# A mixture-of-experts stage with each pair's gate and up products one step ahead of its down products, and five pairs of eight through a table in DRAM

## The chip, the cores and the metric

The kernel runs on one core of a Trainium2 chip. The metric is the device time of one execution in microseconds; a time that stands for a kernel is the median of its runs. The rows come from one profiled execution, and their time starts at the beginning of its span.

## The reference

Two layers, each a token mixer and a mixture of experts, on 256 tokens of 1024 channels, all in float32. The change concerns the experts alone (16 of them with an inner width of 256; each token takes two experts of one group of four):

```python
def moe_ffn(h, w_router, b_router, w_gate, w_up, w_down):
...
    _, local = lax.top_k(in_group, TOP_K_EXPERTS)
...
    gate = jnp.einsum('tk,tke->te', wts, jax.nn.one_hot(expert_idx, N_EXPERTS, dtype=jnp.float32))
    hid = jax.nn.silu(jnp.einsum('td,edf->tef', h, w_gate)) * jnp.einsum('td,edf->tef', h, w_up)
    hid = hid * gate[:, :, None].astype(hid.dtype)
    return jnp.einsum('tef,efd->td', hid, w_down)
...
        y = moe_ffn(h.reshape(bsz * seq, d), w_router, b_router, w_gate[l], w_up[l], w_down[l])
        x = layer_norm(DEEPNORM_ALPHA * x + (1.0 + g_f) * y.reshape(bsz, seq, d), ln_ffn_g[l], ln_ffn_b[l])
```

## The kernel before

The experts of a layer are worked through as eight pairs `p` (`E // 2`). Of a pair, each expert has 64 slots for tokens, so that the two lie side by side on 128 partitions. Per layer the pairs read 33.6 MB of gate and up weights (`w_gu`, 8 loads of 0.524 MB for a pair) and 16.8 MB of down weights (`w_dn`, 4 such loads for a pair).

For each pair the code does this:

- **Gathering** (L1096 to L1111, `gather`): matmuls of 128x256 with a one-hot matrix `oh` bring the tokens of two pairs (`q = p // 2`) into their slots, transposed. One call makes 8 matmuls into a PSUM bank of tag `t` and lets ScalarE (L208) and VectorE (L1110) write two of the eight blocks of `xg`. Four calls, 32 matmuls, serve two pairs. For pairs 4 and 6 they are recorded in the pair ahead (`AHEADP = ((3, 5), (3, 5))`), for pair 2 between its own products.
- **Gate and up products** (L1205): 16 instructions, each run as two matmuls, into one bank of tag `s`.
- **Activation**: three calls on ScalarE (L208), two on VectorE (L1235, L1236).
- **Two transposes** (L1238), a copy by ScalarE to `hdT` (L1240), and **down products** (L1253): 8 instructions, two halves `n` of 512 columns.
- **Output.** For `p < DIRECT = 6`, VectorE multiplies (L1257) and GpSimd stores the half into a table in DRAM (L1258, 0.262 MB a store). Pairs 6 and 7 go directly: one-hot rows (`slot_rows`, L1218), a multiply (L1265), a split into two parts (L418, L419), and matmuls L1278 that add into the four banks `py`.
- **Table rows** (L1148 to L1159, `table_rows`, recorded at `p == DIRECT`): four indirect loads by GpSimd (L1154, 0.524 MB each) read the two rows of every token, and VectorE adds them to `xrow` (eight sums, L1159). At the end `xrow` is added into `py` (L1273, L1274) and the layer norm follows.

The weights come through `Stream`: SP issues all loads (L92) in one list (built at L167 to L189), which for each pair names the gate and up weights and then the down weights. Each load waits until its buffer's last reader is done. Tag `P`, for down weights, has six buffers, tag `ring` has ten. SP executes in order, so that a load that waits holds up all behind it.

A scheduler sets the order of instructions on each engine from the recorded program and priorities; it may move an instruction ahead of one that was recorded earlier. PSUM has four banks of tag `mm`, two of `s`, two of `t`.

Of the kernel before, what the change touches and what calls it, by code (L numbers as in the profile page):

```python
# [11 lines left out]
F32R = mybir.dt.float32r  # L12
# [25 lines left out]

DIRECT = 6

AHEADP = ((3, 5), (3, 5))

# [70 lines left out]
def _trunk(ctx, tc, x_tok, x_chn, par, pos, rows, b_ada, w_ada, w_idx, w_in, w_out, w_gu, w_dn, out):  # L113
# [30 lines left out]
    for l in range(L):  # L144
# [32 lines left out]
        st.add(("gu", l, 2), w_gu[l, 2], 8, which=range(2, 7))  # L177
        for p in range(2, E // 2):
            if p in SP[l]:
                st.add(("gu", l, p), w_gu[l, p], 8, which=range(2))  # L180
                st.add(("gu2", l, p), w_gu[l, p], 4, "S", (2,))
                st.add(("gu", l, p), w_gu[l, p], 8, which=(2, 3, 6, 7))
            elif p > 2:
                st.add(("gu", l, p), w_gu[l, p], 8)
            if p in DNS[l]:
                st.add(("dn", l, p), w_dn[l, p], 4, "P", (0, 1))
                st.add(("dn2", l, p), w_dn[l, p], 2, "S", (1,))
            else:
                st.add(("dn", l, p), w_dn[l, p], 4, "P")  # L189
    norm_rows(2 * L - 1)  # L190
# [666 lines left out]
    for l in range(L):  # L857
# [237 lines left out]

        def gather(xg, q, k0):  # L1096
            pt = ps("t")
            for j in range(2):
                k = k0 + j
                for tt in range(2):  # L1100
                    for i, src in enumerate((xh, xl)):
                        last = PE.matmul(pt[:, j * 256:(j + 1) * 256], src[:, tt * D + k * P:tt * D + (k + 1) * P],  # L1102
                                  oh[:, tt * D + q * 256:tt * D + (q + 1) * 256], start=(tt + i == 0), stop=(tt + i == 2))
            for j in range(2):
                k = k0 + j
                o, t = xg[:, k * 256:(k + 1) * 256], pt[:, j * 256:(j + 1) * 256]
                if j == 0:
                    act(o, t, AF.Identity, scale=gp[:, k:k + 1], bias=bp[:, k:k + 1])
                else:
                    V.tensor_scalar(o, t, gp[:, k:k + 1], bp[:, k:k + 1], op0=OP.mult, op1=OP.add)  # L1110
            return last  # L1111

        xg = sb("S")
        gl = gather(xg, 0, 0)
        for (la, na), q in zip(LAST[l], pa):
# [64 lines left out]

        for p in range(E // 2):
            pgu = ps("s")
            if p and p % 2 == 0 and p - 1 not in AHEADP[l]:
                xg = sb("S")
            elif p % 2 == 0 and p:
                xg = xnext
            if p in AHEADP[l]:
                xnext = sb("S")

            order = (2, 3, 0, 1) if p == 1 else range(4)  # L1190
            for i in order:
                if p == 0 and i or p and p % 2 == 0 and p - 1 not in AHEADP[l]:
                    gather(xg, p // 2, 2 * i)
                if p in AHEADP[l]:
                    gather(xnext, p // 2 + 1, 2 * i)
                if ("gu2", l, p, i) in st.index:
# [5 lines left out]
                for k in range(2):  # L1202
                    for s in range(2):
                        c0 = (2 * i + k) * 256 + p % 2 * P + s * 64
                        PE.matmul(pgu[s * 64:s * 64 + 64, :], xg[:, c0:c0 + 64], ws[s][k],  # L1205
                                  start=(i == order[0] and k == 0), stop=(i == order[3] and k == 1), tile_position=(0, 64 * s))
            if p == 0:
                sgate = slot_gates()
            if p == 1:
                with tc.issue_after(stored.ins):  # L1210
                    affine_rows(xrow, xn, 2 * l, True)
            if p == DIRECT:
                py = [[ps("mm") for _ in range(2)] for _ in range(2)]
                table_rows()
            def slot_rows(pt):

                for s in range(2):
                    PE.matmul(pt[s * 64:s * 64 + 64, 256:512], identb[:, 2 * p + s:2 * p + s + 1].to_broadcast([P, 64]), rankz,  # L1218
                              start=True, stop=True, tile_position=(0, 64 * s))
                ohT = sb("e", F32R)[:, 0:256]  # L1220
                V.tensor_scalar(ohT, pt[:, 256:512], pidx, None, op0=OP.is_equal)
                return ohT

            late = LATE_ROWS[l] or p < DIRECT
            if LATE_ROWS[l]:
                pt = pgu
            else:
                pt = ps("t")
            if not late:
                ohT = slot_rows(pt)  # L1230
            si = sb("rope")[:, 0:256]
            act(si, pgu[:, 0:256], AF.Exp, scale=-1.0)
            act(si, si, AF.Ln, bias=ones)
            act(si, si, AF.Exp, scale=-1.0)
            V.scalar_tensor_tensor(si, pgu[:, 0:256], sgate[:, p:p + 1], si, op0=OP.mult, op1=OP.mult)  # L1235
            V.tensor_tensor(si, pgu[:, 256:512], si, op=OP.mult)  # L1236
            for j in range(2):
                PE.transpose(pt[:, j * P:(j + 1) * P], si[:, j * P:(j + 1) * P], ident)  # L1238
            hdT = sb("sg")[:, 0:256].rearrange("p (j t) -> p j t", j=2)
            A.copy(hdT, pt[:, 0:256].rearrange("p (j t) -> p j t", j=2))  # L1240
            if late and p >= DIRECT:
                ohT = slot_rows(pt)
            for n in range(2):
# [4 lines left out]
                else:  # L1248
                    wd = [parts_of(("dn", l, p, 2 * n + s)) for s in range(2)]
                pyb = ps("t" if p >= DIRECT else "mm")  # L1250
                for k in range(2):
# [117 lines left out]
```

## Time and profile before

| | us |
|---|---|
| median of 3 runs | 732.42 |
| lowest and highest | 731.96, 732.84 |
| the profiled execution | 735.13 |
| its span | 733.4 |
| TensorE busy | 662.6 (90%) |
| VectorE busy | 404.1 (55%) |

The experts of layer 0 run from about 242 to 375 us of the span, those of layer 1 from about 592 to the end. A busy share is an average over stages with different limits, so the stages are read one by one: windows tell what is busy in a stretch, the waits of SP tell whether a load was held up by a reader of its buffer or by earlier loads that had not landed, and the chain of waits tells which work ended last.

### The profile page before, as it was taken

How to read it: one execution, taken by the hardware profiler on the slowest of the kernel's cores; microseconds unless marked ns; L12 is line 12 of the kernel's file. 1: busy time of each engine (PE TensorE's matmuls, PEld its weight loads, DVE VectorE, ACT ScalarE, POOL GpSimd, SP SyncE). 2: the span in 40 equal slices, each digit the busy share in tenths (PEclk: the TensorE clock that was granted, in tenths of full speed). 3: DMA queues.
4: the chain of work that ended last, by engine and by line, in shares of the span. 5: the costliest groups of instructions: out<-in, count | busy, mean ns of one | idle time of the engine just before them, and what ended most of it. 6: DMA issues, size and time to landing. Idle time of an engine off the chain costs nothing. (4 is left out here: it accounts for less than half of the span.)

```text
span 733.4 us, 10314 instructions
## 1 busy us (share of the span) xinstructions
PE 662.6 (90%) x3578; PEld 402.0 (55%) x3578; DVE 404.1 (55%) x882; ACT 274.2 (37%) x571; POOL 209.7 (29%) x207
## 2 busy tenths in 40 slices
PE   5899699999998999999778999999799799999863
PEld 0567587864775443442246679886377644434222
DVE  5478996653985322221387999664745622222236
ACT  3346658344323212120146646844432222211112
POOL 5003934001922054003034513400830304510201
PEclk9999989999897999999989999999989699999997
DMA  8997773499987799999944774439958569999971
GB/s 305 408 365 239 259 259 119 150 364 409 384 294 252 272 371 339 374 414 412 409 181 142 253 250 147 155 100 373 368 209 255 198 230 329 344 367 412 412 287 57
DMA packets 58849, 210.25 MB, mean 287 GB/s; under 512 B 6948, under 2 KB 7076, under 8 KB 57511
## 3 DMA queue, kind: packets, MB, share of 16 engines
q1 hardware_dynamic: 55152, 198.49, 74.2%
q0 software_dynamic: 3200, 10.50, 3.6%
q8 instruction: 30, 0.49, 0.3%
q10 hardware_dynamic: 438, 0.54, 0.2%
q14 instruction: 29, 0.23, 0.1%
HBM read 202.15 MB, written 7.35 MB: 286 GB/s over the span
## 5 line engine op out<-in xcount | busy, mean ns | idle before, releaser
L419 DVE TENSOR_TENSOR sb_w<-sb_ring,sb_w 128x512 fp32r<-128x512 f32 (+1 forms) x156 | 121.5, 791 | 40.5 <-ACT sb_w L418 39.2
L418 ACT CAST sb_w<-sb_ring 128x512 fp32r<-128x512 f32 (+1 forms) x156 | 92.2, 608 | 82.2 <-PE ps_mm L438 43.6
L1205 PE MATMUL ps_s<-sb_ring,sb_S 128*64 128x512 f32 x424 | 118.3, 611 | 4.5 <-DMA sb_ring<-w_gu 4.2
L437 PE MATMUL ps_mm<-sb_w,sb_H 128*128 128x512 f32 (+2 forms) x224 | 81.3, 368 | 1.1 <-ACT sb_w L418 0.7
L438 PE MATMUL ps_mm<-sb_w,sb_H 128*128 128x512 f32 (+2 forms) x224 | 79.5, 357 | 2.9 <-DVE sb_H L891 2.8
L439 PE MATMUL ps_mm<-sb_w,sb_H 128*128 128x512 f32 (+2 forms) x224 | 73.7, 372 | 2.1 <-DVE sb_w L419 2.0
L1205 PEld LDWEIGHTS ps_s<-sb_ring,sb_S 128*64 128x64 f32 x424 | 32.2, 138 | 65.3 <-issue 44.6
L920 POOL TENSOR_TENSOR sb_ring<-sb_ring,sb_g 128x512 f32<-128x512 f32 x32 | 46.8, 1500 | 66.9 <-DMA sb_ring<-w_out 66.9
L1258 POOL DMA_DIRECT2D table<-sb_e x24 | 13.4, 558 | 174.0 <-DVE sb_e L1257 154.4
L352 PE MATMUL ps_t<-sb_ring,cact 128*32 128x512 f32 x272 | 46.1, 616 | 8.2 <-DVE cact L218 6.7
L1110 DVE TENSOR_SCALAR sb_S<-ps_t,afffg,afffb 128x256 f32<-128x256 f32 x32 | 17.4, 544 | 62.0 <-ACT sb_S L208 62.0
L439 PEld LDWEIGHTS ps_mm<-sb_w,sb_H 128*128 128x128 f32 x224 | 40.8, 194 | 15.4 <-DVE sb_w L419 6.7
L437 PEld LDWEIGHTS ps_mm<-sb_w,sb_H 128*128 128x128 f32 x224 | 42.8, 193 | 11.4 <-issue 3.1
L438 PEld LDWEIGHTS ps_mm<-sb_w,sb_H 128*128 128x128 f32 x224 | 43.0, 193 | 8.9 <-DVE sb_H L891 3.6
L1253 PE MATMUL ps_mm<-sb_P,sb_sg 128*64 128x512 f32 x176 | 46.2, 597 | 0.7 <-ACT sb_sg L1240 0.5
L1102 PEld LDWEIGHTS ps_t<-sb_O,sb_H 128*128 128x128 f32 x256 | 33.0, 193 | 19.0 <-issue 13.0
L208 ACT ACTIVATE sb_S<-ps_t,afffb,afffg 128x256 f32<-128x256 f32 x32 | 18.1, 564 | 62.3 <-PE ps_t L1102 62.3
L438 PE MATMUL ps_mm<-sb_H,sb_w 128*128 128x256 f32 x128 | 37.2, 291 | 3.9 <-DVE sb_w L419 3.9
L531 POOL TENSOR_TENSOR sb_rope<-sb_rope 128x256 f32<-128x256 f32 (+1 forms) x16 | 14.2, 888 | 92.7 <-DVE iwm L567 32.7
L636 POOL TENSOR_SCALAR sb_sg<-sb_sg,sm 128x128 f32<-128x128 f32 (+1 forms) x32 | 27.6, 880 | 45.6 <-DVE sm L633 31.7
L1102 PE MATMUL ps_t<-sb_O,sb_H 128*128 128x256 f32 x256 | 38.7, 297 | 1.8 <-DVE sb_O L1032 1.8
L1235 DVE SCALAR_TENSOR_TENSOR sb_rope<-ps_s,sgate,sb_rope 128x256 f32<-128x256 f32 x16 | 7.7, 482 | 53.1 <-ACT sb_rope L208 53.1
(368 smaller groups left out, 1243.8 us busy)
## 6 DMA issues: line engine op xcount, KB each, us to landing
sb_ring<-w_gu SPq DMA_DIRECT2D x106, 512.0 KB, 7.0
sb_ring<-w_ada SPq DMA_DIRECT2D x96, 512.0 KB, 5.7
sb_P<-w_dn SPq DMA_DIRECT2D x58, 512.0 KB, 11.4
sb_ring<-w_in SPq DMA_DIRECT2D x56, 512.0 KB, 4.4
sb_ring<-w_out SPq DMA_DIRECT2D x16, 512.0 KB, 10.0
sb_S<-w_gu SPq DMA_DIRECT2D x6, 1024.0 KB, 5.7
table<-sb_e POOLq DMA_DIRECT2D x24, 256.0 KB, 6.5
sb_row<-rows SPq DMA_DIRECT2D x8, 512.0 KB, 10.2
```

What stands on the lines that cost most here:

```text
L208: return A.activation(o, i, f, bias=bias, scale=scale)
L352: PE.matmul(pa[32 * g:32 * g + 32, :], cact[:, k:k + 1].to_broadcast([P, 32]), w[g // 2][:, (g % 2) * 512:(g % 2) * 512 + 512], start=(i = ...
L418: A.copy(hi, src)
L419: V.tensor_tensor(lo, src, hi.bitcast(F32), op=OP.subtract)
L437: PE.matmul(o, a[0], b[0], start=start, stop=False)
L438: PE.matmul(o, a[1], b[0], start=False, stop=False)
L439: return PE.matmul(o, a[0], b[1], start=False, stop=stop)
L636: G.tensor_scalar(sg[:, i * n:(i + 1) * n], sg[:, i * n:(i + 1) * n], sm[:, h:h + 1], None, op0=OP.mult)
L920: G.tensor_tensor(q, q, g1[l][0][:, n * 512:(n + 1) * 512], op=OP.mult)
L1102: last = PE.matmul(pt[:, j * 256:(j + 1) * 256], src[:, tt * D + k * P:tt * D + (k + 1) * P], oh[:, tt * D + q * 256:tt * D + (q + 1) * 25 ...
L1205: PE.matmul(pgu[s * 64:s * 64 + 64, :], xg[:, c0:c0 + 64], ws[s][k], start=(i == order[0] and k == 0), stop=(i == order[3] and k == 1), ti ...
L1253: PE.matmul(pyb[s * 64:s * 64 + 64, :], hdT[:, k, s * 64:s * 64 + 64], wd[s][k], start=(k == 0), stop=(k == 1), tile_position=(0, 64 * s))
```

## The change

- The loop over pairs becomes a loop over nine steps. A step records the gate and up products of pair `step` and their activation, then, for pair `p = step - 1`, the transposes, the copy, the whole gathering for pair `p + 2` (where `p` is even), and the down products. `AHEADP` is gone.
- The gathering for pairs 0 and 1 is recorded ahead of their products (the first call aside, which was there before).
- `gather` uses banks of tag `mm` (its first call `t`), the down products of all pairs `t`.
- The list of weights names the gate and up weights of pair `p` ahead of the down weights of pair `p - 1`.
- `DIRECT` is 5: five pairs are stored in the table, pairs 5, 6 and 7 go directly.

```diff
-DIRECT = 6
-
-AHEADP = ((3, 5), (3, 5))
+DIRECT = 5
...
-        for p in range(2, E // 2):
-            if p in SP[l]:
+        for p in range(3, E // 2 + 1):
+            if p == E // 2:
+                pass
+            elif p in SP[l]:
...
-            if p in DNS[l]:
-                st.add(("dn", l, p), w_dn[l, p], 4, "P", (0, 1))
+            if p - 1 in DNS[l]:
+                st.add(("dn", l, p - 1), w_dn[l, p - 1], 4, "P", (0, 1))
...
-        def gather(xg, q, k0):
-            pt = ps("t")
+        def gather(xg, q, k0, tag="mm"):
+            pt = ps(tag)
...
-        for p in range(E // 2):
+        def gate_up(p):
+
             pgu = ps("s")
-            if p and p % 2 == 0 and p - 1 not in AHEADP[l]:
-                xg = sb("S")
-            elif p % 2 == 0 and p:
-                xg = xnext
-            if p in AHEADP[l]:
-                xnext = sb("S")
...
+        for i in range(1, 4):
+            gather(xg, 0, 2 * i)
+
+        now = []
+        for step in range(E // 2 + 1):
+            if step < E // 2:
+                pgu = gate_up(step)
+                if step == 0:
+                    sgate = slot_gates()
+                now.append((pgu, activation(step, pgu)))
+            if step == 0:
+                continue
+            p = step - 1
+            pgu, si = now.pop(0)
+            pt = pgu if LATE_ROWS[l] else ps("t")
+            for j in range(2):
+                PE.transpose(pt[:, j * P:(j + 1) * P], si[:, j * P:(j + 1) * P], ident)
+            hdT = sb("sg")[:, 0:256].rearrange("p (j t) -> p j t", j=2)
+            A.copy(hdT, pt[:, 0:256].rearrange("p (j t) -> p j t", j=2))
+            if p % 2 == 0 and p < E // 2 - 2:
+                xg = sb("S")
+                for i in range(4):
+                    gather(xg, p // 2 + 1, 2 * i)
...
-                pyb = ps("t" if p >= DIRECT else "mm")
+                pyb = ps("t")
```

In the changed program the lines move: gate and up products L1196, activation L1205 and L1206 on VectorE, transposes L1234, copy L1236, down products L1259, multiply and store L1263 and L1264, direct products L1284, loads on SP L90. The lines up to L1166 that are named above (L1102, L1154, L1159) keep their numbers.

**TensorE, layer 1, around pair 2's down products.** Before, from the gathering behind pair 1's down products on (`sb_O` is the one-hot gathering's operand, `sb_sg` is `hdT`, `sb_P` the down weights, `ident` marks transposes):

```order
L1102 MATMUL ps_t<-sb_O,sb_H 128x256 x16
L1205 MATMUL ps_s<-sb_ring,sb_S 64x512 x4
L1205 MATMUL ps_s<-sb_S 64x512 x4
L1205 MATMUL ps_s<-sb_ring,sb_S 64x512 x4
L1102 MATMUL ps_t<-sb_O,sb_H 128x256 x5
L1238 MATMUL ps_s<-ident,sb_rope 128x128 x2
L1102 MATMUL ps_t<-sb_O,sb_H 128x256 x11
L1253 MATMUL ps_mm<-sb_P,sb_sg 64x512 x8
L1205 MATMUL ps_s<-sb_ring,sb_S 64x512 x7
```

After:

```order
L1259 MATMUL ps_t<-sb_w,sb_sg 64x512
L1196 MATMUL ps_s<-sb_ring,sb_S 64x512 x8
L1196 MATMUL ps_s<-sb_S 64x512 x4
L1196 MATMUL ps_s<-sb_ring,sb_S 64x512 x4
L1234 MATMUL ps_s<-ident,sb_rope 128x128 x2
L1102 MATMUL ps_mm<-sb_O,sb_H 128x256 x24
L1259 MATMUL ps_t<-sb_P,sb_sg 64x512 x8
L1196 MATMUL ps_s<-sb_ring,sb_S 64x512 x16
L1234 MATMUL ps_s<-ident,sb_rope 128x128 x2
```

The down products of pair 2 stand behind 24 gather products that follow its transposes; counted from the start of the layer's experts, 104 gather products stand ahead of them, before 88. In layer 0 the same count is 64 before and 88 after, and two more gate and up instructions of pair 4.

**SP, layer 1, the loads of the experts from their third pair on.** Before:

```order
L92 DMA sb_O<-w_gu 128x2048
L92 DMA sb_ring<-w_gu 128x1024 x10
L92 DMA sb_S<-w_gu 128x2048
L92 DMA sb_P<-w_dn 128x1024 x4
L92 DMA sb_ring<-w_gu 128x1024 x2
L92 DMA sb_P<-w_dn 128x1024 x2
L92 DMA sb_ring<-w_gu 128x1024 x9
L92 DMA sb_P<-w_dn 128x1024 x4
L92 DMA sb_ring<-w_gu 128x1024 x8
```

After:

```order
L90 DMA sb_O<-w_gu 128x2048
L90 DMA sb_ring<-w_gu 128x1024 x10
L90 DMA sb_S<-w_gu 128x2048
L90 DMA sb_P<-w_dn 128x1024 x4
L90 DMA sb_ring<-w_gu 128x1024 x5
L90 DMA sb_P<-w_dn 128x1024 x2
L90 DMA sb_ring<-w_gu 128x1024 x6
L90 DMA sb_P<-w_dn 128x1024 x4
L90 DMA sb_ring<-w_gu 128x1024 x8
```

Two down loads move back by three ring loads; the four down loads that go into the buffers freed by pair 2's down products (the last row but one) keep their place in the stream of bytes. So does the last gate and up load of each layer, which is followed by four down loads (2.1 MB) in layer 1 and two (1.0 MB) in layer 0.

**TensorE, layer 1, late: pairs 4 and 5.** Before, from pair 5's transposes (the last stored pair) to pair 6's transposes:

```order
L1238 MATMUL ps_s<-ident,sb_rope 128x128 x2
L1205 MATMUL ps_s<-sb_ring,sb_S 64x512 x3
L1253 MATMUL ps_mm<-sb_P,sb_sg 64x512 x4
L1205 MATMUL ps_s<-sb_ring,sb_S 64x512 x8
L1253 MATMUL ps_mm<-sb_P,sb_sg 64x512 x4
L1238 MATMUL ps_s<-ident,sb_rope 128x128 x2
```

After, from the last gate and up products ahead of pair 4's down products (now the last stored pair) to pair 5's first:

```order
L1196 MATMUL ps_s<-sb_ring,sb_S 64x512 x7
L1259 MATMUL ps_t<-sb_P,sb_sg 64x512 x4
L1196 MATMUL ps_s<-sb_ring,sb_S 64x512 x4
L1259 MATMUL ps_t<-sb_P,sb_sg 64x512 x4
L1234 MATMUL ps_s<-ident,sb_rope 128x128 x2
L1212 LDWEIGHTS identb
L1212 MATMUL ps_s<-rankz,identb 64x256
L1212 LDWEIGHTS identb
L1212 MATMUL ps_s<-rankz,identb 64x256
L1259 MATMUL ps_t<-sb_P,sb_sg 64x512 x4
```

The last stored down products stand 5.2 MB earlier in the stream of weights than before, and 3.1 MB earlier in layer 0 (counted by the last weights that TensorE needs up to them). On VectorE the eight sums L1159 stand behind pair 7's last multiply in both programs (six in a row, then two between the subtractions), and on TensorE of layer 0 the direct products of pair 6 now stand ahead of pair 7's last three gate and up instructions.

## Rows read from the trace of the kernel before

**Rows 1.** The page, 40 slices of 18.3 us: GB/s moved.

```profile
GB/s 305 408 365 239 259 259 119 150 364 409 384 294 252 272 371 339 374 414 412 409 181 142 253 250 147 155 100 373 368 209 255 198 230 329 344 367 412 412 287 57
```

**Rows 2.** Windows: busy PE, PEld, DVE, ACT, POOL (counts); clock, DMA share, GB/s.

```profile
290.00:300.00 10.00, 10.00 (x55) 4.88 (x55) 3.02 (x5) 1.74 (x4) 1.10 (x2) 1.00 0.93 325
...
370.00:380.00 10.00, 10.00 (x36) 5.01 (x35) 8.00 (x14) 3.69 (x9) 1.78 (x3) 0.75 0.14 30
...
640.00:650.00 10.00, 10.00 (x49) 3.82 (x49) 3.17 (x6) 1.81 (x5) 1.11 (x2) 1.00 0.93 309
```

**Rows 3.** DMA view of 310 to 335 us.

```profile
DMA packets 2715, 10.32 MB, mean 413 GB/s; under 512 B 326, under 2 KB 326, under 8 KB 2586
```

**Rows 4.** SP's waits, 286-301, 310-343, 640-648, 655-695: total us, times, longest.

```profile
SPq L92 <- PE ps_s L1205: 6.7, 3, 3.2
SPq L92 <- PE ps_mm L1253: 5.1, 2, 4.2
...
SPq L92 <- DMA sb_ring<-w_gu: 16.5, 15, 1.7
...
SPq L92 <- PE ps_mm L1253: 4.2, 2, 3.3
...
SPq L92 <- DMA sb_ring<-w_gu: 21.5, 20, 2.1
```

**Rows 5.** SP's timeline: start us, us, loads issued.

```profile
242.46 0.33 SPq L92 DMA_DIRECT2D sb_O<-w_gu  x1
...
292.48 2.96 SPq L92 DMA_DIRECT2D sb_P<-w_dn  x4
...
301.51 6.47 SPq L92 DMA_DIRECT2D sb_ring<-w_gu  x8
...
339.13 1.61 SPq L92 DMA_DIRECT2D sb_ring<-w_gu  x2
...
642.90 2.62 SPq L92 DMA_DIRECT2D sb_P<-w_dn  x4
```

**Rows 6.** TensorE's timeline (one row), then two rows of the chain of waits.

```profile
354.25 3.45 PE L1205 MATMUL ps_s<-sb_ring,sb_S 128*64 128x512 f32 x6 [1.38 <-DMA sb_ring<-w_gu]
...
701.02 1.95 PE ps_s L1205 x6
...
712.59 3.02 DVE sb_X L1159 x5
```

**Rows 7.** TensorE's timeline: start us, us, matmuls, [idle before <-releaser].

```profile
242.50 2.17 PE L1102 MATMUL ps_t<-sb_O,sb_H 128*128 128x256 f32 x16
...
253.32 3.65 PE L1205 MATMUL ps_s<-sb_ring,sb_S 128*64 128x512 f32 x16
...
289.20 0.44 PE L1238 MATMUL ps_t<-ident,sb_rope 128*128 128x128 f32 x2 [1.76 <-DVE sb_rope L1236]
```

**Rows 8.** GpSimd's timeline; DMA view of 348-356 and 697-705 (median us to landing).

```profile
343.27 1.11 POOL L1154 DMA_INDIRECT sb_H<-table,which  x1 [6.20 <-DMA table<-sb_e]
...
347.31 0.99 POOL L1154 DMA_INDIRECT sb_H<-table,which  x1 [0.30 <-issue]
...
696.93 0.99 POOL L1154 DMA_INDIRECT sb_H<-table,which  x1 [0.30 <-issue]
...
q0 software_dynamic: 447, 1.63, 51.3%
...
sb_H<-table,which POOLq DMA_INDIRECT x1, 11.6
...
sb_H<-table,which POOLq DMA_INDIRECT x1, 11.1
```

**Rows 9.** The transposes L1238: their engine idle before them (us, times) until.

```profile
  DVE sb_rope L1236: 10.2, 8
```

**Rows 10.** VectorE's timeline: a direct pair's multiply and subtraction.

```profile
698.82 0.69 DVE L1265 TENSOR_TENSOR sb_e<-ps_t,sb_g 128x512 f32<-128x512 f32 x1 [6.76 <-PE ps_t L1253]
700.20 0.69 DVE L419 TENSOR_TENSOR sb_w<-sb_e,sb_w 128x512 fp32r<-128x512 f32 x1 [0.69 <-ACT sb_w L418]
```

More of the change, by code (lines that the diff above doesn't have):

```diff
@@ L182, in _trunk @@
                 st.add(("gu", l, p), w_gu[l, p], 8, which=(2, 3, 6, 7))
-            elif p > 2:
+            else:
                 st.add(("gu", l, p), w_gu[l, p], 8)
-            if p in DNS[l]:
-                st.add(("dn", l, p), w_dn[l, p], 4, "P", (0, 1))
-                st.add(("dn2", l, p), w_dn[l, p], 2, "S", (1,))
+            if p - 1 in DNS[l]:
+                st.add(("dn", l, p - 1), w_dn[l, p - 1], 4, "P", (0, 1))
+                st.add(("dn2", l, p - 1), w_dn[l, p - 1], 2, "S", (1,))
             else:
-                st.add(("dn", l, p), w_dn[l, p], 4, "P")
+                st.add(("dn", l, p - 1), w_dn[l, p - 1], 4, "P")
     norm_rows(2 * L - 1)
@@ L1113, in _trunk @@
         xg = sb("S")
-        gl = gather(xg, 0, 0)
+        gl = gather(xg, 0, 0, "t")
         for (la, na), q in zip(LAST[l], pa):
@@ L1179, in parts_of @@
             return [w[:, k * 512:(k + 1) * 512] for k in range(2)]
-        for p in range(E // 2):
+        def gate_up(p):
             pgu = ps("s")
-            if p and p % 2 == 0 and p - 1 not in AHEADP[l]:
-                xg = sb("S")
-            elif p % 2 == 0 and p:
-                xg = xnext
-            if p in AHEADP[l]:
-                xnext = sb("S")
             order = (2, 3, 0, 1) if p == 1 else range(4)
             for i in order:
[L1192 to L1195, printed above, removed]
                 if ("gu2", l, p, i) in st.index:
@@ L1206, in _trunk, with activation, slot_rows @@
                                   start=(i == order[0] and k == 0), stop=(i == order[3] and k == 1), tile_position=(0, 64 * s))
-            if p == 0:
-                sgate = slot_gates()
+            return pgu
+        def activation(p, pgu):
+            si = sb("rope")[:, 0:256]
+            act(si, pgu[:, 0:256], AF.Exp, scale=-1.0)
+            act(si, si, AF.Ln, bias=ones)
+            act(si, si, AF.Exp, scale=-1.0)
+            V.scalar_tensor_tensor(si, pgu[:, 0:256], sgate[:, p:p + 1], si, op0=OP.mult, op1=OP.mult)
+            V.tensor_tensor(si, pgu[:, 256:512], si, op=OP.mult)
+            return si
+        def slot_rows(p, pt):
+            for s in range(2):
+                PE.matmul(pt[s * 64:s * 64 + 64, 256:512], identb[:, 2 * p + s:2 * p + s + 1].to_broadcast([P, 64]), rankz,
+                          start=True, stop=True, tile_position=(0, 64 * s))
+            ohT = sb("e", F32R)[:, 0:256]
+            V.tensor_scalar(ohT, pt[:, 256:512], pidx, None, op0=OP.is_equal)
+            return ohT
+        for i in range(1, 4):
[20 more added lines that the diff above has]
+                    gather(xg, p // 2 + 1, 2 * i)
             if p == 1:
@@ L1214, in _trunk @@
                 table_rows()
[L1215 to L1242, printed above, removed]
+            if p >= DIRECT:
+                ohT = slot_rows(p, pt)
             for n in range(2):
```

## The prediction

> **What bounds the kernel now.** I read the slices of the page first. In the two stretches of the experts' work (slices 13 to 20 and 32 to 39) the transfer rate is uneven: 198 to 272 GB/s at the start of each, 409 to 414 near its end [rows 1]. The windows say the same finer: at 290 to 300 us TensorE is busy all the time while the transfers reach 325 GB/s, and likewise 309 at 640 to 650; between 310 and 335 the mean is 413 GB/s [rows 2, 3]. So each stretch has two regimes, first TensorE, then the transfers.
>
> The waits of SP, which issues all weight loads in one order, show where the first regime ends. Up to 301 us it waits for products to free buffers: 6.7 us for gate and up products, 5.1 for down products; from 310 on it waits for landings (16.5 us for the ring alone). In layer 1 it waits 4.2 us for down products around 642.9, and from 655 on for landings (21.5 us) [rows 4]. Its last long wait for TensorE ends at 301.51 in layer 0 (the third ring load after the four down loads of 292.48) and at 642.90 in layer 1 [rows 5].
>
> What ends a layer is the landing of the last gate and up weights of pair 7: in layer 0 the last six matmuls start at 354.25 after a wait for such a load; in layer 1 the chain of waits goes through them at 701.02, then to the sums L1159 at 712.59 [rows 6]. These follow pair 7's multiply on VectorE in both programs. So the question is when the last 0.5 MB of gate and up weights lands, and this time passes to the end unchanged: at 370 to 380 the transfers are busy 0.14 only, so nothing is buffered that could take up a delay of layer 0 [rows 2].
>
> By the order listing the last gate and up load stands at the same place of the byte stream before and after. Counted from the loads in SP's row (0.524 MB each, 1.05 for tags O and S), 36.2 MB are issued from 242.46 up to the end of this load in layer 0; 16.3 MB stand ahead of the loads of 292.48, and 19.4 MB ahead of 301.51. In layer 1, 16.3 MB stand ahead of 642.90.
>
> **The change, part by part.** *(a) Gathering ahead of down products.* Pair 2's down products read the buffers into which SP's next down loads go, and all later loads stand behind these on SP. In layer 0, 64 gather products stand ahead of them now and 88 then, and two more gate/up instructions (two matmuls each). A gather matmul takes 2.17/16 = 0.136 us, a gate/up matmul 3.65/16 = 0.228 [rows 7]: 24 x 0.136 + 4 x 0.228 = 4.2 us later. Against it, the transposes no longer come straight after the activation; their wait for L1236 there was 1.76 us [rows 7], which the next pair's products now fill. Net 2.4: the down loads go from 292.5 to 294.9. Then all 36.2 - 16.3 = 19.9 MB follow at 0.413 MB/us [rows 3]: 294.9 + 48.2 = 343.1. Now the last stop is 301.51 with 16.8 MB to come: 301.5 + 40.7 = 342.2. (Stores and table rows come on top of both.) So +0.9 us. In layer 1 the gather products ahead go from 88 to 104: 16 x 0.136 = 2.2 us, on the stop that binds already, so +2.2. Bounds: none of it, if enough is outstanding to bridge the stop; or 4.2 in layer 0 with no wait saved, which gives 344.9 there, +2.7. I take 0.9 and 2.2, since at 640 to 650, around this stop, the rate falls to 309 now [rows 2]: the stop isn't bridged.
>
> *(b) Fewer stores.* One pair fewer goes through DRAM: two stores of 0.262 MB fewer per layer. In layer 0 six stores lie behind the binding stop either way (pairs 3 to 5 behind 301.5; pairs 2 to 4 behind 294.9): 0. In layer 1 eight become six: -0.52/0.413 = -1.3 us.
>
> *(c) Table rows earlier.* The four indirect loads L1154 (0.524 MB each, 2.1 in all) are issued once the last store has landed, at 343.27 to 347.31 in layer 0 and until 696.93 in layer 1; the last of them lands 11.6 and 11.1 us later, at 358.9 and 708.0. While they run they take half of the transfers' time (51.3%) [rows 8], 0.207 MB/us. So they move 4.65 x 0.207 = 0.96 MB behind 354.25, and 7.0 x 0.207 = 1.45 MB behind 701.02, where no weight waits for them. In the changed order the last stored pair is pair 4; its down weights stand 3.1 MB (layer 0) and 5.2 MB (layer 1) further ahead in what TensorE needs, 7 to 12 us at 0.413. I take it that the indirect loads start about 8 us earlier, so that all of their bytes run ahead of the last gate and up weights, which then land later by 0.96/0.413 = 2.3 and 1.45/0.413 = 3.5 us. Earlier rows gain nothing, because the sums L1159 stay behind pair 7's multiply. Bounds: 0 (they start no earlier) and these 5.8.
>
> *(d) What I cost at nothing.* The activation's wait (10.2 us over eight places [rows 9]) beyond the 1.76 above: it lies mostly where landings bind, and the transfers hide it. The gathers' bank and the down products' bank: both swap places among the same six banks. Pair 5's direct products (eight L1284 instead of two multiplies and stores) lie in the stretch bound by transfers. One cover may be gone: in layer 0 pair 6's L1284 products now stand ahead of pair 7's last three gate/up instructions; they wait for a multiply, a cast and a subtraction, 0.69 us each [rows 10], and less than 0.6 us of products stands in between, so up to 1.5 us, and as much in layer 1. I take 0, since the weights of the products behind land later than those of pair 6's down products.
>
> The profile speaks against filling TensorE's gaps here: they are short where TensorE binds. The Trainium skill, "Perfetto Trace Analysis", section "Optimization Strategy", says that where the most contended engine changes over time "performance may be improved by interleaving those regimes". Rows 2 and 3 show these regimes, and the change does the reverse: gathering goes from the second into the first. By that rule it loses up to what it moves, 24 and 16 gather products, 3.3 and 2.2 us; my sum, with the bytes, has 0.9 and 2.2.
>
> **Sum.** Layer 0: 0.9 + 0 + 2.3 = +3.2. Layer 1: 2.2 - 1.3 + 3.5 = +4.4. Together +7.6 on the profiled execution of 735.13: 742.7. Its time is 2.7 us over the median of the runs (732.42), so the forecast of the median is 740.0.
>
> **The rivals.** *A, faster: the freed wait counts and the rest is hidden.* If over 1 MB is outstanding when pair 2's down buffers come free, SP's later issue starves nothing; what then binds in layer 0 is the ring release of 301.5, which comes some 1.5 us earlier because the 1.76 us wait is filled. Only pairs 3 and 4 store behind it (-1.3 in each layer), and the table rows start no earlier. -1.5 - 1.3 - 1.3 = -4.1: 728.3. For it: from 310 and 655 on SP waits for landings alone [rows 4], so there something is outstanding. Against it: the rate falls at just that stop. The Trainium skill's section "Optimization Strategies" of the same page makes it the goal to keep the matmul engine from idling; by it all 10.2 us would be a gain, 722, but rows 4 show SP waiting for landings in most of that time.
>
> *B, no change: the change doesn't do what it says.* The scheduler puts the next pair's products ahead of the down products already in before (the order rows show it), so overlap isn't new; if the stop is bridged and the rows start only 4 us earlier in layer 0, +1.2 - 1.3 remains: 732.3.
>
> *C, slower by more.* The lateness in layer 0 is not reduced (+2.7 instead of +0.9), and TensorE stands behind L1284 for 1.5 us in each layer: 740.0 + 1.8 + 3.0 = 744.8.
>
> **How the numbers follow.** Forecast 0.54 (740.0), A 0.20 (728.3), B 0.14 (732.3), C 0.12 (744.8). Low end: stores gain in both layers, all else is hidden, 732.4 - 2.6 = 729.8, so 730; high end C, 745. A alone lies outside for the most part. About 0.2% (1.5 us) is what a measurement of this kernel can tell from no change: slower 0.66 (forecast and C), same 0.14 (B), faster 0.20 (A).
>
> **What would show it.** For (a): SP waiting for L1259 right ahead of the third group of down loads, ending near 295 and near 645, and a rate at 640 to 650 below 309. For (c): L1154 issued near 335 and 685, landed before the last gate and up weights, and these at about 357.5 and 705.4. For (d): no wait for VectorE or ScalarE on TensorE between pair 6's and pair 7's products. The prediction is wrong if the SP stop vanishes from the first regime, if the last gate/up weights land before 354 and 701, or if the sums L1159 run ahead of pair 7's multiply.

## The result

The changed kernel takes 742.7 us (median of 4 runs, 739.31 to 746.5), the kernel before 732.25 (4 runs). The ratio is 1.0143, with a 95% interval of 1.0111 to 1.0174: slower by some 10 us. Measured once more beside other kernels (e11 below) it took 745.67 us, a ratio of 1.0175 [1.0142, 1.0208]. The profiled execution took 743.76 us (span 742.1), 8.6 more than that of before.

The windows around the down loads, the first pair for layer 0's first ones (before, then changed), the other two of the changed kernel, against [rows 2] (TensorE's clock is the third figure from the end, the transfers' GB/s the last):

```profile
260.00:270.00 10.00, 9.54 (x48) 3.78 (x47) 3.53 (x6) 2.49 (x6) 4.68 (x5) 1.00 0.97 353
...
260.00:270.00 10.00, 10.00 (x59) 5.62 (x58) 4.22 (x8) 3.60 (x8) 0.88 (x2) 1.00 0.60 207
...
290.00:300.00 10.00, 10.00 (x56) 4.44 (x56) 3.67 (x7) 1.63 (x3) 1.08 (x2) 1.00 0.80 281
...
640.00:650.00 10.00, 10.00 (x60) 5.20 (x58) 3.72 (x7) 3.12 (x7) 1.08 (x2) 1.00 0.94 347
```

Such a window is fixed while the stages shift, so it doesn't show by itself how deep a hole in the transfers is: from 280 to 310 us the mean is 367 GB/s, and 370 before. Counted from the stage's first load, layer 0 moves 363 GB/s in its first 110 us and 372 before, which is 1.0 MB less, or 2.4 us at 0.413 MB/us. About half of it is missing after 50 us, by an earlier stop: pair 0's down products now stand behind the gathering for pair 2, and SP's first down loads go 25.0 us after the first load instead of 20.7. The other half goes in the 10 us from 50 to 60, around the stop that the prediction priced (274 GB/s, 327 before). In layer 1 there is no such difference (364 and 365 GB/s).

SP's wait for down products (286 to 298; total us, times, longest) and below it its timeline show the stops, against [rows 4, 5]. The second fence has two rows of the kernel before:

```profile
SPq L90 <- PE ps_t L1259: 7.1, 2, 6.2
```

```profile
242.01 0.33 SPq L90 DMA_DIRECT2D sb_O<-w_gu  x1
...
267.01 3.00 SPq L90 DMA_DIRECT2D sb_P<-w_dn  x4
...
294.56 2.83 SPq L90 DMA_DIRECT2D sb_P<-w_dn  x4
...
594.59 0.34 SPq L90 DMA_DIRECT2D sb_O<-w_gu  x1
...
646.04 3.65 SPq L90 DMA_DIRECT2D sb_P<-w_dn  x4
```

```profile
263.19 5.76 SPq L92 DMA_DIRECT2D sb_P<-w_dn  x6
...
591.28 0.34 SPq L92 DMA_DIRECT2D sb_O<-w_gu  x1
```

The down loads behind pair 2's products go out at 294.56 in layer 0. In layer 1 they go 51.5 us after the stage's first load (594.59), in the kernel before 51.6 (591.28 to 642.90). GpSimd's timeline shows the first table load 7 and 11 us earlier than before, where it goes at 343.27 [rows 8] and, the last row here, at 692.92:

```profile
336.11 1.12 POOL L1154 DMA_INDIRECT sb_H<-table,which  x1 [6.91 <-issue]
...
682.24 1.09 POOL L1154 DMA_INDIRECT sb_H<-table,which  x1 [6.42 <-issue]
...
692.92 1.09 POOL L1154 DMA_INDIRECT sb_H<-table,which  x1 [6.96 <-DMA table<-sb_e]
```

TensorE's timeline at the end of layer 0, against the first of [rows 6], holds the main news:

```profile
351.39 2.41 PE L1259 MATMUL ps_t<-sb_P,sb_sg 128*64 128x512 f32 x8 [1.27 <-DMA sb_P<-w_dn]
354.76 1.46 PE L1284 MATMUL ps_mm<-sb_w,sb_e 128*128 128x512 f32 x4 [0.95 <-ACT sb_w L418]
356.15 1.50 PE L1259 MATMUL ps_t<-sb_P,sb_sg 128*64 128x512 f32 x5
...
359.51 0.73 PE L1284 MATMUL ps_mm<-sb_w,sb_e 128*128 128x512 f32 x2 [1.43 <-ACT sb_w L418]
360.18 1.93 PE L1196 MATMUL ps_s<-sb_ring,sb_S 128*64 128x512 f32 x6
362.04 0.73 PE L1284 MATMUL ps_mm<-sb_w,sb_e 128*128 128x512 f32 x2
364.64 0.41 PE L1234 MATMUL ps_t<-ident,sb_rope 128*128 128x128 f32 x2 [1.87 <-DVE sb_rope L1206]
```

Before, pair 7's last six gate and up matmuls waited for a landing. Now no landing stands ahead of them: they wait behind pair 6's direct products L1284, and these for ScalarE's cast of pair 6's second half, which itself could only be multiplied after down products that stood behind the first half's direct products. Layer 1 does the same, in the chain of waits:

```profile
698.91 1.95 PE ps_t L1259 x6
700.88 0.70 DVE sb_e L1271
701.60 0.63 ACT sb_w L418
702.27 1.46 PE ps_mm L1284 x4
703.73 1.43 PE ps_t L1259 x5
...
705.63 0.70 DVE sb_e L1271
706.36 0.63 ACT sb_w L418
707.03 0.73 PE ps_mm L1284 x2
707.76 1.86 PE ps_s L1196 x6
...
714.60 0.45 PE ps_s L1234 x2
```

Two rounds of product, multiply, cast and direct product, one after the other, and only then pair 7's last products. Pair 7's transposes of the kernel before, to set against those at 364.64 and 714.60:

```profile
360.15 0.44 PE L1238 MATMUL ps_t<-ident,sb_rope 128*128 128x128 f32 x2 [0.28 <-DVE sb_rope L1236]
...
705.40 0.44 PE L1238 MATMUL ps_s<-ident,sb_rope 128*128 128x128 f32 x2 [1.31 <-DVE sb_rope L1236]
```

### The profile page after: what moved, and what is told of

Same layout as the page of the kernel before. It is cut to its first block, busy times and chain, and to the rows that moved or that the text cites. A ratio compares the mean times of both kernels' runs of the same rounds, so it can differ in the third digit from the quotient of the medians.

```text
span 742.1 us, 10366 instructions
## 1 busy us (share of the span) xinstructions
PE 667.2 (90%) x3598; PEld 406.5 (55%) x3598; DVE 409.8 (55%) x888; ACT 275.5 (37%) x575; POOL 207.2 (28%) x203
## 5 line engine op out<-in xcount | busy, mean ns | idle before, releaser
L1196 PE MATMUL ps_s<-sb_ring,sb_S 128*64 128x512 f32 x424 | 116.5, 600 | 2.4 <-DMA sb_ring<-w_gu 1.9
L1259 PE MATMUL ps_t<-sb_P,sb_sg 128*64 128x512 f32 x232 | 64.4, 613 | 3.2 <-DMA sb_P<-w_dn 2.3
L1196 PEld LDWEIGHTS ps_s<-sb_ring,sb_S 128*64 128x64 f32 x424 | 32.7, 136 | 63.1 <-issue 47.5
L1264 POOL DMA_DIRECT2D table<-sb_e x20 | 11.1, 557 | 153.1 <-DVE sb_e L1263 134.8
L208 ACT ACTIVATE sb_rope<-ps_s 128x256 f32<-128x256 f32 x16 | 6.2, 384 | 122.6 <-PE ps_s L1196 122.6
L1205 DVE SCALAR_TENSOR_TENSOR sb_rope<-ps_s,sgate,sb_rope 128x256 f32<-128x256 f32 x16 | 7.7, 482 | 79.0 <-ACT sb_rope L208 79.0
L439 PEld LDWEIGHTS ps_mm<-sb_w,sb_H 128*128 128x128 f32 x224 | 41.7, 197 | 14.7 <-DVE sb_w L419 5.4
L437 PEld LDWEIGHTS ps_mm<-sb_w,sb_H 128*128 128x128 f32 x224 | 43.7, 197 | 9.9 <-issue 3.2
L438 PEld LDWEIGHTS ps_mm<-sb_w,sb_H 128*128 128x128 f32 x224 | 44.0, 197 | 9.1 <-DVE sb_H L891 3.7
L438 PE MATMUL ps_mm<-sb_H,sb_w 128*128 128x256 f32 x128 | 38.1, 298 | 2.7 <-DVE sb_w L419 2.7
L437 PE MATMUL ps_mm<-sb_H,sb_w 128*128 128x256 f32 x128 | 37.6, 295 | 0.0
L439 PE MATMUL ps_mm<-sb_H,sb_w 128*128 128x256 f32 x128 | 37.6, 294 | 0.0
L1259 PEld LDWEIGHTS ps_t<-sb_P,sb_sg 128*64 128x64 f32 x232 | 18.1, 140 | 34.6 <-issue 24.8
## 6 DMA issues: line engine op xcount, KB each, us to landing
sb_row<-rows SPq DMA_DIRECT2D x8, 512.0 KB, 10.2
```

Of the source, the lines that this page charges most:

```text
L437: PE.matmul(o, a[0], b[0], start=start, stop=False)
L438: PE.matmul(o, a[1], b[0], start=False, stop=False)
L439: return PE.matmul(o, a[0], b[1], start=False, stop=stop)
L1259: PE.matmul(pyb[s * 64:s * 64 + 64, :], hdT[:, k, s * 64:s * 64 + 64], wd[s][k], start=(k == 0), stop=(k == 1), tile_position=(0, 64 * s))
```

## The experiments

Theory 1: the changed kernel loses by what stands ahead of pair 7's last gate and up products, namely bytes (table rows, down loads late) and TensorE's place behind pair 6's direct products. Theory 2: the pipelined order, gathering ahead of the down products, is the loss by itself. Each kernel is compared with the kernel before, run on the same chip beside it; runs of one kernel scatter by 3 to 7 us, and the intervals take that in.

**e1, the pipelined order with six stored pairs.**

```diff
-DIRECT = 5
+DIRECT = 6
```

> The changed kernel with DIRECT back at 6: the pipelined order alone, pair 5 through the table again. Theory 1 (the changed kernel loses by what stands ahead of pair 7's last gate and up weights: the table rows moved ahead of them, 2.3 and 3.5 us, and the direct products of pairs 5 and 6, which hold TensorE up, 1.3 and 3.0 us by the spans of its trace): the table rows start late again (near 344 and 695), so that most of these 10.1 us return, less 1.3 us a layer for two more stores: 735 to 738. Theory 2 (the loss is the pipelined order itself, gathering ahead of the down products): 741 to 744, unchanged.

Measured: 738.48 us, 1.0074 [1.0044, 1.0103]. Half of the loss goes, half stays. TensorE's and GpSimd's timelines of e1:

```profile
357.51 1.93 PE L1196 MATMUL ps_s<-sb_ring,sb_S 128*64 128x512 f32 x6 [0.36 <-DMA sb_ring<-w_gu]
...
342.73 1.12 POOL L1154 DMA_INDIRECT sb_H<-table,which  x1 [6.22 <-DMA table<-sb_e]
```

The last six products wait for a landing again, and the table loads start as late as before. Yet the landing is later than before: 357.51 against 354.25 (3.8 us more when both are counted from the stage's first load). With the steps of the prediction that is lateness 0.9, two more stores behind the earlier stop 1.3, and table rows of which more now run ahead of a later landing 1.9: 4.1. (The last step is reckoned with the measured landing, so the sum isn't a free forecast of it.) In layer 1 of e1 no product waits for a landing, and pair 7's transposes come only 0.2 us later than before.

**e2, the old order with five stored pairs.**

```diff
-DIRECT = 6
+DIRECT = 5
```

> The kernel before with DIRECT at 5 and nothing else: pair 5 direct, in the old order. Theory 1: the table rows start 5 to 8 us earlier than 343 and 693 and move ahead of pair 7's last gate and up weights, +2 to +5.8 us, pair 5's direct products add up to 4 us of waiting on TensorE, two stores fewer give back 1.3 to 2.6: 735 to 740. Theory 2: with the order of before it stays at 731 to 733.

Measured: 739.14 us, 1.0072 [1.0046, 1.0098]. So the two parts of the change cost about the same alone, and 0.74% and 0.72% add up to what both cost together (1.43% and 1.75% in its two measurements). Theory 2 alone can't be right. The parts are not independent, though: e4 and e6 below compare the two orders once more. TensorE in e2, once in each layer:

```profile
357.24 1.93 PE L1205 MATMUL ps_s<-sb_ring,sb_S 128*64 128x512 f32 x6 [0.22 <-DMA sb_ring<-w_gu]
...
705.47 0.73 PE L1278 MATMUL ps_mm<-sb_w,sb_e 128*128 128x512 f32 x2 [0.88 <-ACT sb_w L418]
706.14 1.93 PE L1205 MATMUL ps_s<-sb_ring,sb_S 128*64 128x512 f32 x6
```

In layer 0 the landing sets the products, 1.2 us later from the stage's first load (the steps: table rows 2.3, stores -1.3). In layer 1 the direct products do, though the order is the old one.

**e3, the table loads held.** GpSimd copies one column of pair 6's activation before it issues the loads:

```diff
+                wait = wk.tile([P, 1], F32, name="wait", tag="wait")
+                table_rows(G.tensor_copy(wait, now[0][1][:, 0:1]))
...
+                    with tc.issue_after(held.ins):
+                        G.indirect_dma_start(out=r[:, o], out_offset=None, in_=table[l],
```

> The changed kernel, in which GpSimd copies one column of pair 6's activation ahead of the four table loads, so that these start when pair 6's activation is done (about 343 in layer 0 and 688 in layer 1 instead of 336 and 682). Theory 1: half or more of the rows' bytes run behind pair 7's last gate and up weights again, which land 2 to 5 us earlier in all: 737 to 741. Theory 2 (the transfers had room, TensorE's direct products alone set the time): 742 to 743.

Measured: 738.37 us, 1.0066 [1.0041, 1.0092]. Starting the rows at 342.5 instead of 336.1 returns about half of the loss: the bytes count. But TensorE still stands behind the casts (waits of 1.08 and 1.43 us, in the changed kernel 0.95 and 1.43), only earlier, since pair 6's down weights land earlier too:

```profile
342.48 1.13 POOL L1155 DMA_INDIRECT sb_H<-table,which  x1 [1.09 <-issue]
...
355.71 0.73 PE L1286 MATMUL ps_mm<-sb_w,sb_e 128*128 128x512 f32 x2 [1.43 <-ACT sb_w L418]
356.38 1.93 PE L1197 MATMUL ps_s<-sb_ring,sb_S 128*64 128x512 f32 x6
```

**e4, pair 6's direct products behind pair 7's products.**

```diff
-                        tail = PE.matmul(py[tt][n], o if len(parts) == 2 else o.bitcast(F32), y, start=...
+                        with tc.issue_after(gate_up.last.ins) if p == 6 else nullcontext():
+                            tail = PE.matmul(py[tt][n], o if len(parts) == 2 else o.bitcast(F32), y, start=...
```

> The changed kernel, in which pair 6's eight direct products are issued behind pair 7's last gate and up product on TensorE instead of between them. Theory 1: pair 7's last products follow the landing of their weights (356.5 and 706.6 in the trace of the changed kernel) instead of 360.2 and 710.2; the trace's two layers lost 1.3 and 3.0 us there, so 738 to 739. Theory 2 (the landing sets the end and TensorE catches up): 742 to 743.

Measured: 735.76 us, 1.0030 [1.0013, 1.0046]. Nothing but the place of sixteen instructions on one engine changed, and most of the loss is gone, more than I expected. TensorE, end of layer 0 and of layer 1:

```profile
351.92 4.07 PE L1259 MATMUL ps_t<-sb_P,sb_sg 128*64 128x512 f32 x13 [1.42 <-DMA sb_P<-w_dn]
...
357.04 1.93 PE L1196 MATMUL ps_s<-sb_ring,sb_S 128*64 128x512 f32 x6 [0.20 <-DMA sb_ring<-w_gu]
358.90 2.14 PE L1285 MATMUL ps_mm<-sb_w,sb_e 128*128 128x512 f32 x8
361.51 0.41 PE L1234 MATMUL ps_t<-ident,sb_rope 128*128 128x128 f32 x2 [0.47 <-DVE sb_rope L1206]
...
703.81 1.93 PE L1196 MATMUL ps_s<-sb_ring,sb_S 128*64 128x512 f32 x6 [0.21 <-DMA sb_ring<-w_gu]
...
708.19 0.44 PE L1234 MATMUL ps_s<-ident,sb_rope 128*128 128x128 f32 x2 [0.41 <-DVE sb_rope L1206]
```

Thirteen of pair 6's sixteen down products run in one row that no direct products interrupt, pair 7's last products follow their landing, and the direct products fill the time of pair 7's activation. Pair 7's transposes come 119.5 and 117.0 us after their stage's first load (242.06 and 591.18), in the changed kernel 122.6 and 120.0: 3.2 and 3.0 us of standing behind direct products.

**e5, gathering behind the down products of its step.**

```diff
-            if p % 2 == 0 and p < E // 2 - 2:
-                xg = sb("S")
-                for i in range(4):
-                    gather(xg, p // 2 + 1, 2 * i)
...
+                with tc.issue_after(down.ins):
+                    for i in range(4):
+                        gather(xg, p // 2 + 1, 2 * i)
```

> The changed kernel, in which each gathering is issued behind the down products of its step instead of ahead of them (in layer 0, 64 gather products ahead of pair 2's down products, in the changed kernel 88). Theory 1 (lateness of the down buffers is a small part, 0.9 us in layer 0, and near 0 in layer 1 where the trace shows the down loads at the same distance from the stage's first load): SP's third group of down loads goes out near 290 instead of 294.6, the last gate and up weights land 1 to 2 us earlier, 740 to 742. Theory 2 (gathering ahead of the down products is the main cost): back to 733 to 736. If the next pair's products now wait for their gathered tokens, slower than 743.

Measured: 737.17 us, 1.0077 [1.0051, 1.0103], between the theories. It doesn't decide: more than the gathering moved with it. SP's stop for the down products shrinks to 2.8 us in two waits (the down loads go at 288.39), but the ring loads then wait for gate and up products that now come after the gathering: 9.5 us over four waits, the longest 5.3, until 296.22. And fewer casts are waited for in layer 1 (0.6 us instead of 2.4).

**e6, e2 with pair 6's direct products behind pair 7's products.** They are kept in a list and issued after pair 7's last gate and up product:

```diff
+            if p == 7:
+                with tc.issue_after(last_gu.ins):
+                    for q, o, y, first in held:
+                        PE.matmul(q, o, y, start=first, stop=False)
...
+                        if p == 6:
+                            held.append((py[tt][n], o, y, p == DIRECT and m == 0))
+                            continue
```

> The kernel before with five stored pairs, and pair 6's direct products behind pair 7's last gate and up product. Theory 1 (the cost of five stored pairs is that TensorE stands behind direct products, in the old order as in the new): layer 1, where TensorE waited 2.3 us for casts and the stage was 5.5 us longer, loses 3 of them: 734 to 737 against 739 with the products in between. Theory 2 (the table rows moved ahead are the cost): unchanged, 738 to 740.

Measured: 734.44 us, 1.0022 [0.9995, 1.0049], against 1.0072 for e2. The old order loses and regains by the same place on TensorE, so the direct products are the cost of five stored pairs, not of the pipelining; the table rows ahead of the landing remain and weigh little here. With the direct products late, the order of gathering and down products makes no difference that the runs can tell: e4 (pipelined) 1.0030, e6 (old order) 1.0022, and with early sums e8 0.9968, e10 0.9964 below. In the traces the landing of layer 0 is still 2.7 us later in e4 than in e6. So that the pipelining costs 0.7% holds for e1 beside the kernel before, and not for every program; why it is more there than in e4 stays open.

**e7, the kernel before with early sums.** In both layers the eight sums L1159 had stood at the very end, six of them in a row [rows 6]. The first line is the kernel before; an edge on VectorE now puts four ahead of pair 7's activation and four ahead of its first multiply:

```profile
712.50 3.69 DVE L1159 TENSOR_TENSOR sb_X<-sb_X,sb_H 128x512 f32<-128x512 f32 x6
```

```diff
+            with tc.issue_after(table_rows.half.ins) if p == 7 else nullcontext():
+                V.scalar_tensor_tensor(si, pgu[:, 0:256], sgate[:, p:p + 1], si, op0=OP.mult, op1=OP.mult)
...
+                with tc.high_priority(offset=AHEAD_SPLIT), tc.issue_after(table_rows.last.ins) if p == 7 else nullcontext():
+                    V.tensor_tensor(yg, pyb, g1[l][1][:, n * 512:(n + 1) * 512], op=OP.mult)
```

> The kernel before, in which VectorE does the first four sums L1159 ahead of pair 7's activation and the other four ahead of pair 7's first multiply. The sums leave the end of each layer, where six of them take 3.7 us in a row between the multiply and the split of the sums: if that row of VectorE sets the end, 2.5 to 4 us less per layer, 725 to 728. If the rows land too late for it (358.9 and 708.1, 1.3 and 1.9 us ahead of the multiply) VectorE is held up instead: 732 to 735.

Measured: 725.36 us, 0.9921 [0.9885, 0.9957], as expected.

**e8, e4 with all eight sums ahead of pair 7's activation.**

```diff
+            with tc.issue_after(table_rows.last.ins) if p == 7 else nullcontext():
+                V.scalar_tensor_tensor(si, pgu[:, 0:256], sgate[:, p:p + 1], si, op0=OP.mult, op1=OP.mult)
```

> The changed kernel with pair 6's direct products behind pair 7's last gate and up product (as in e4) and all eight sums ahead of pair 7's activation on VectorE. In e4 the table rows landed at 352 and 696, long ahead of it, so nothing is held up: what five stored pairs make possible is used. 2.5 to 4 us less per layer than e4: 728 to 731 against 735.8. If something else sets the end of the layer (the split, the layer norm), 735.

Measured: 729.97 us, 0.9968 [0.9944, 0.9993], as expected, and 4.6 us behind e7.

**e9, e7 with the last four sums behind both operations of pair 7's activation.**

```diff
+            act7 = V.tensor_tensor(si, pgu[:, 256:512], si, op=OP.mult)
+            if p == 7:
+                with tc.issue_after(act7.ins):
+                    for o, r in table_rows.rest:
+                        table_rows.last = V.tensor_tensor(xrow[:, o], xrow[:, o], r[:, o], op=OP.add)
```

> The kernel before, as in e7, but the last four sums stand behind both operations of pair 7's activation on VectorE (ahead of its first multiply). In e7 the second of these operations waited in layer 1 behind sums whose rows landed at 700.5 and 703.0, so that the transposes of pair 7 came 6.8 us after its last product instead of 3.6. If the rest holds, 2 to 4 us less than e7: 721 to 724. If the sums then hold up the multiply by as much, 725, unchanged.

Measured: 722.5 us, 0.9867 [0.9837, 0.9898]: faster than both kernels. VectorE at the end of layer 1:

```profile
698.35 1.29 DVE L1245 TENSOR_TENSOR sb_X<-sb_X,sb_H 128x512 f32<-128x512 f32 x2 [0.44 <-DMA sb_H<-table,which]
700.88 1.29 DVE L1245 TENSOR_TENSOR sb_X<-sb_X,sb_H 128x512 f32<-128x512 f32 x2 [1.24 <-DMA sb_H<-table,which]
...
702.61 0.69 DVE L1274 TENSOR_TENSOR sb_e<-ps_t,sb_g 128x512 f32<-128x512 f32 x1
```

The sums wait for their rows while TensorE works on pair 7's down products, and next to nothing waits for the sums: pair 7's first multiply comes 3.6 us after the first of these down products (699.00), in the kernel before 3.5. TensorE's wait for the casts ahead of the `xrow` matmuls, 4.77 and 4.74 us before, is down to 0.25 and 0.24.

**e10, e6 with all sums ahead of pair 7's activation**, by the edit of e8.

> The kernel e6 (order of before, five stored pairs, pair 6's direct products behind pair 7's last product) with all eight sums ahead of pair 7's activation. Its rows landed at 352 and 695.5, 3 us and more ahead of pair 7's activation, so nothing is held up: 3.5 to 4.5 us a layer less than e6, 725 to 727. If five stored pairs with early sums are worth more than six (fewer stores, no wait for rows), 722.

Measured: 730.12 us, 0.9964 [0.9944, 0.9984], 3 us above the range. The sums could have run when the rows had landed, but they stand behind pair 6's split on VectorE, and pair 7's activation behind them:

```profile
701.21 0.69 DVE L419 TENSOR_TENSOR sb_w<-sb_e,sb_w 128x512 fp32r<-128x512 f32 x1 [0.69 <-ACT sb_w L418]
701.82 4.90 DVE L1159 TENSOR_TENSOR sb_X<-sb_X,sb_H 128x512 f32<-128x512 f32 x8
```

A part of the 4.9 us only moved from one side of the activation to the other: TensorE's wait for pair 7's activation grows from 0.41 us to 2.04 and 3.25, while its wait of some 4.8 us at the end of each layer goes, and e10 is 4.3 us faster than e6. The part that moved is the same mistake as that of the changed kernel, on another engine.

**e11, the changed kernel again**, without an edit.

> The changed kernel as it is, beside the two above on the same chip. If the loss is in the program and not in a run, 739 to 746 again, with TensorE waiting for the casts of pair 6's direct products (about 2.4 us in each layer) behind the landing of pair 7's last gate and up weights.

Measured: 745.67 us, 1.0175 [1.0142, 1.0208], with the same waits for casts: 2.4 us of them in layer 0 and 2.9 in layer 1.

## Why the prediction was right in direction and size, and where its sum was wrong

The median, 742.7, lies between the forecast (740.0) and rival C (744.8). The direction and the size came out, but the size by luck. With the direct products out of the way (e4), everything that the sum had priced at 7.6 us costs 0.30% in the runs, some 2 us; what it had costed at nothing costs 1.1%, some 8 us. The two errors nearly cancel.

- **The bound** held where a landing is the last wait: the last gate and up weights of pair 7 set the end of each stage in the kernel before, in e4 and e6, and of layer 0 in e1 and e2. In the changed kernel something later took over. That such a delay "passes to the end unchanged" did not hold: the landings of e4 are 3.2 and 2.9 us later than before, 6.1 together, and its span grows by 1.9.
- **(a) Lateness.** Layer 0: the down loads were forecast for 294.9 and went at 294.56. But the sum counted from the last stop alone. The earlier one at pair 0's down products, 4.3 us later from the stage's first load, costs bytes too, and once the transfers bind they are not made up: the lateness by bytes is 2.4 us where the sum had 0.9, within its bound of 2.7. Landings agree: e4's is 2.7 us behind e6's, and these differ by the order alone. Layer 1: forecast 2.2 us later, measured 0.2 earlier. The 16 more gather products are there (80 in 10.2 us instead of 64 in 8.7), but the 64 gate and up products among them take 13.9 us instead of 15.2, since they now run in unbroken rows. The rate at 640 to 650 rose to 347 GB/s, against the prediction's sign, in a fixed window while the stage starts 3.3 us later.
- **(b) and (c) Bytes.** The table loads were forecast near 335 and 685 and went at 336.1 and 682.2. In layer 0 the steps of the sum can be set against the four kernels whose last products waited for the landing (from the first load of the stage, in us later than before): e1 4.1 by the steps and 3.8 measured, e2 1.0 and 1.2, e4 3.2 and 3.2, e6 1.0 and 0.5. In layer 1, without (a), they give 2.2 for e4 and e6, measured 2.9 and 1.3. So the sums come out within about 1 us. Their parts do not all: rows less stores are 0.5 and 1.3 us in e6 where the steps give 1.0 and 2.2, and in layer 0 of the changed kernel the order makes up for it. By e4 the landings cost about 6 us where I had 7.6.
- **(d) Costed at nothing** is the step that failed. I saw that pair 6's direct products stood ahead of pair 7's last products, bounded that by 1.5 us a layer from one multiply, cast and subtraction, and took 0 because the weights behind land later. Measured: 3.2 and 3.0 us up to pair 7's transposes (e4), 1.1% in the runs. Two things were missing. There are two rounds, one for each half, and the second half's down products stand behind the first half's direct products. And the landing doesn't cover them. Placed by e4, it comes at 357.0 in layer 0 and 707.2 in layer 1. In layer 0 the first round ends ahead of it, but the second round's direct products come at 359.51, and six products of pair 7 behind them. In layer 1 fourteen products of pair 7 stand behind the rounds, six at 707.69 and eight at 710.21; eight of the fourteen need not wait for this landing and could have started at 704.7, placed by e4 too.
- **TensorE's clock in layer 0.** 3.2 us of landing and 3.2 of direct products make 6.4, but the transposes come only 4.9 us later. In the kernel before the last six gate and up matmuls took 3.45 us (0.58 each) [rows 6], in the changed one 1.93 (0.32): the first stood in a stretch with a granted clock of 0.83, so in part at the level of 1.2 GHz, the second in one of 1.00, 2.4 GHz (first row before, second changed):

```profile
350.00:360.00 10.00, 7.88 (x22) 2.64 (x19) 3.05 (x6) 1.93 (x4) 0.00 (x0) 0.83 1.03 409
...
360.00:370.00 10.00, 6.94 (x30) 2.41 (x28) 3.31 (x7) 2.30 (x5) 0.00 (x0) 1.00 1.03 410
```

  That is 1.5 us in favour of the changed kernel, in this one execution of the kernel before; whether its clock fell there in the others, no trace shows.
- **What came back.** Up to pair 7's transposes the two layers lose 4.9 and 5.9 us in the trace, 10.8 together. The span grew by 8.7 only: 0.5 were gained ahead of the first stage, 1.2 behind the transposes of layer 0 and 0.5 behind those of layer 1. Most of layer 0's lies in its last products, which took 7.4 us at a granted clock of 0.75 [rows 2] before and 6.4 at 0.83 now. In layer 1 two of the sums, contrary to what I wrote ahead of the result, ran ahead of pair 7's first multiply, at 719.05, and TensorE's wait for the cast behind them fell from 4.74 to 3.89 us:

```profile
716.43 1.28 DVE L1159 TENSOR_TENSOR sb_X<-sb_X,sb_H 128x512 f32<-128x512 f32 x2
```

- **Rival A** failed at the point that it named: SP's stop stayed. **Rival B** failed with e1 and e2: each part alone is slower by 0.7%. **Rival C** named the right mechanism (TensorE behind L1284) at half its price, and its lateness of 2.7 in layer 0 is near the 2.4 measured.

The Trainium skill, "Perfetto Trace Analysis", section "Optimization Strategy", says that interleaving regimes may improve the time where the most contended engine changes; the change did the reverse. In layer 0 the traces agree: pair 2's down products start 2.6 us later from the stage's first products, and the order costs 2.4 us. In layer 1 the down loads went no later, and with the direct products late the runs can't tell the two orders apart (e4 and e6). The Trainium skill's section "Optimization Strategies" of the same page asks, where the matmul engine idles waiting for others, to optimize the engines that hold it up. In the changed kernel its waits for casts are 2.4 us in each layer, but moving the products that wait returned 3 us and more: the products queued behind a wait are part of its price, and the wait's own figure doesn't hold them.

Open: e1's profile is 2.1 us over that of before, its median 5.5, and e4 regained 8 us and more in the runs, where the traces show 6.8. The profiled execution of the kernel before took 2 to 3 us more than its medians, which explains a part of both. The rest lies within the scatter of single executions (734.1 to 741.0 for e1), and I can't place it.

## What to carry to other kernels

On an engine that runs in order, a step that needs two other engines must not stand between products that are ready: put it where the next wait is anyway, here behind pair 7's last products, in the time of pair 7's activation. When a chain of short steps is bounded, count its rounds and what each round holds up, not one wait. When a later issue of loads is priced, count every stop ahead of the stretch in which the transfers bind, not the last alone. And before moving work forward, look at what the end of the stage does in a row: the eight sums that stood at the end of each layer of the kernel before, six of them in a row, were worth 10 us (e9), as much as the whole change cost.

## What the runs showed of the hardware that I had not expected

A gather matmul of 128x256 takes less time in a long row than in a short one, and so does a gate and up matmul. Gather matmuls in layer 1 of the kernel before, then of the changed one:

```profile
616.96 0.50 PE L1102 MATMUL ps_t<-sb_O,sb_H 128*128 128x256 f32 x2
```

```profile
641.04 3.11 PE L1102 MATMUL ps_mm<-sb_O,sb_H 128*128 128x256 f32 x24
```

A row's length holds the end of its last matmul, which overlaps the next row, so these are counted from start to start: a gather matmul takes 0.22 us in the row of 2 (616.96 to 617.39) and 0.13 in the row of 24 (641.04 to 644.08), a gate and up matmul 0.50 in the row of 2 (617.39 to 618.40) and 0.22 in a row of 32. What the change between kinds of products costs there isn't shown by an experiment of its own. The stretch from the second gathering to pair 2's down products takes 31.6 us in both kernels (609.35 to 640.94, 612.47 to 644.08), with 64 gather products in the one and 80 in the other.

And TensorE's clock differs between kernels in the same place. In the last gate and up products of layer 0, e5's granted clock fell to 0.83 too, where eight matmuls took 4.00 us (0.5 each); in the changed kernel it stayed at 1.00 through 350 to 370 us. In the 20 us before, TensorE was busy 9.7 and 9.1 of 10 us in the kernel before and 9.7 and 9.2 in the changed one, and from 350 to 360 less in the changed one (6.4 of 10 us, against 7.9). These rows don't tell why the one fell and the other didn't.
